# A two-layer decoder step: late gates from SBUF, key-value weights ahead of the norm's root, fewer products for the first sum of squares, denser state steps, outputs in three parts

## The chip, the cores and the metric

The kernel runs on one core of a Trainium2 chip. The metric is device time in microseconds (us) of one execution; lower is better. PE is TensorE (matrix products), DVE is VectorE, ACT is ScalarE, POOL is GpSimd, SP is SyncE, which issues most of the DMAs.

## The reference

One inference step of a hybrid trunk of two layers, for a prompt of 256 tokens behind 16 meta tokens and for 8 single-token samples: 280 columns in all, model width 2048, branch width 4096. Layer A is RWKV-7 time mixing, layer B sliding-window attention with grouped heads; both read one shared key and value. Cut to what the change touches:

```python
def rmsnorm(x, g):
    xf = x.astype(jnp.float32)
    y = xf * lax.rsqrt(jnp.mean(xf * xf, axis=-1, keepdims=True) + RMS_EPS)
    return (y * g.astype(jnp.float32)).astype(x.dtype)
...
    y = (y - mean) * lax.rsqrt(var + GN_EPS) * gn_g.astype(f32).reshape(hn) + gn_b.astype(f32).reshape(hn)
    y = y + jnp.sum(r_h * k_h * r_k.astype(f32), axis=-1, keepdims=True) * v_h
    y = y.reshape(B, T, WIDTH).astype(dt) * jax.nn.silu(z)
    return y @ w_out, S_fin.astype(S0.dtype), xn[:, -1]
...
    kv = (rmsnorm(h, kv_norm) @ w_kv).reshape(B, T, 2, N_KV_HEADS, HEAD_DIM)
    return rotary(kv[:, :, 0], pos), kv[:, :, 1]
...
    y_prompt = rmsnorm(hp, final_norm)[:, N_META:]
    y_sample = rmsnorm(hs, final_norm)
```

The step also returns the new RWKV state of each sample, S x decay - sa x b + v x k, here called a state step.

## The kernel before

Activations lie transposed: model rows on the 128 partitions, the 280 columns along the free axis. KT = 16 tiles of 128 rows make the model width. Matrices are multiplied in three fp32r products, high by high, high by low and low by high (mm3, L205). A weight comes in units of 256 KB (two k tiles by 256 columns): SP loads raw, ACT casts whi (L184), DVE subtracts to get wlo (L186). The buffers of raw, whi and wlo are five units deep, so PE can be some units behind the loads. gemm (L211) runs two units at a time over two banks, one for each 128 columns.

*Order.* In layer A a planner (drive, L591) merges the products with the other streams on PE by written numbers; in the late gates, out_a, phase_b and out_b a scheduler sets the order of each engine ahead of time from the written order and its own costs. At run time each engine's queue is strictly in order: an instruction that waits holds up all behind it.

*Start.* phase0 (L294) squares the 16 tiles of x, adds some squares on DVE and sums the rest over partitions by fp32 products with ones into ps_ssq (L324). A fp32 product counts as two instructions in the profile. Ln and Exp on ACT (L346, L347) give rsb; every first product of PE depends on it. Products of a constant (ps_fill, L320) surround the sums.

*Late gates.* group_norm (L1219) finishes four heads' rows at a time: the bonus tile vT (name 'bonus', two tiles of 272 prompt columns each) takes the normed y (L1237), and SP stores it to yd in DRAM (L1240). gate_a (L1350) loads blocks of 4 x 280 back as gy. For blocks 6 and 7, whose z comes late, it also loads gz from zd, copies the samples' columns from ys (L1362) and multiplies gy with gz on DVE (L1364). gate_tiles splits gy into ghi (ACT) and glo (DVE). At that time PE works on the output projection's first part (ps_o, weights oa1), whose sums into xr (L766, DVE) free its banks. The gates themselves are first used one column later, in out_a.

*out_a* (L1385) runs 8 column pairs of 8 units. After each pair hT is summed (L1404), and kvh, kvl, the parts of the key-value input, are made. Beside it run the state steps of the samples: plan_states gives to each of 12 tiles a unit at which it is computed on DVE (state_step, five instructions); its load is seven units earlier, its store 14 later. The norm's root rb needs the sum of squares of all of hT (ps_sta, L1414): Ln and Exp at L1416 and L1417. Then phase_b multiplies w_kv; bmh and bml (L1424, L1425) are the next layer's inputs, cosr and sinr carry rb into the rotated keys (rout_k, L1651).

*Tail.* out_b (L1800) transposes the last h back (ps_h, L1828), multiplies by the final norm's weight into ht (L1831), sums the squares by ps_stb (L1834), takes a root on DVE (rsf, L1839 and L284 to L288) and scales and stores: 128 prompt rows by DVE and SP (L1844, L1845), 128 by ACT and its own queue (L1846, L1847), the 8 samples last.

## Time and profile before

| what | us |
|---|---|
| three runs | 2165.62, 2161.58, 2156.39 |
| median | 2161.58 |
| the profiled execution | 2157.39 |
| its span (granted TensorE clock 0.993) | 2155.6 |
| DVE busy | 1709.1 |
| ACT busy | 1260.4 |
| DMA moved | 448.52 MB, mean 208 GB/s |

The page shows the busy time of each engine, then the span in 40 slices, the DMA queues, the chain of work that ended last, and the costliest groups. The chain of the whole run is 59% PE. A timeline row gives start and length in us, the engine, the source line, the operation, the tile written and the tiles read, the shape, how many of them, and in brackets how long the engine idled before it and for whom. In the late-gate stage PE stops at 1300.4 us; the root of the key-value norm stands at 1418.9, the last product at 2143.8.

### The profile page before, as it was taken

The numbers are of one execution on the slowest core, as the hardware profiler recorded it, in microseconds if no ns is written. First come the engines' busy times: TensorE is split into PE (matmuls) and PEld (weight loads), VectorE is DVE, ScalarE is ACT, GpSimd is POOL, SyncE is SP. The second block draws the span as 40 slices with busy tenths as digits, with TensorE's granted clock in tenths as the row PEclk, the third lists the DMA queues.
The fourth block names the chain that finished last, engine by engine and source line by source line (L and its number), as shares of the span: only waits on it lengthen the run. The fifth ranks groups of instructions, "written<-read, shape, count | busy, mean of one in ns | idle before, by whom it ended". The sixth has DMA issues, their size and how long they took to land.

```text
span 2155.6 us, 56147 instructions
## 1 busy us (share of the span) xinstructions
PE 2102.4 (98%) x21556; PEld 2001.5 (93%) x21556; DVE 1709.1 (79%) x4115; ACT 1260.4 (58%) x2756; POOL 136.4 (6%) x196
## 2 busy tenths in 40 slices
PE   9999999999999999999999999999999999999997
PEld 7999999999898898889989999999999999999997
DVE  7867867787587777888988787897888888878885
ACT  3457756576666666767666444565565565544443
POOL 0011100001010010100101000100000000000000
PEclk9999999999999999999999999999999999999999
DMA  7997667768666775677655778767545444577774
GB/s 252 310 331 244 197 197 237 207 191 274 200 177 183 249 231 168 208 217 205 199 159 199 242 231 250 238 198 232 149 136 167 153 148 137 170 216 239 230 222 133
DMA packets 277445, 448.52 MB, mean 208 GB/s; under 512 B 53352, under 2 KB 99112, under 8 KB 276784
## 3 DMA queue, kind: packets, MB, share of 16 engines
q1 hardware_dynamic: 276888, 443.89, 66.1%
q8 instruction: 169, 2.77, 0.5%
q10 hardware_dynamic: 288, 1.05, 0.1%
q14 instruction: 100, 0.82, 0.1%
HBM read 382.81 MB, written 66.15 MB: 208 GB/s over the span
## 4 chain that ended last, share of the span: by engine, by line
PE 59%; DVE 4%; DMA 2%; ACT 2%; issue 2%; SPq 0%; DVEq 0%; POOLq 0%; ACTq 0%
PE ps_z L207 5%; PE ps_z L208 5%; PE ps_z L209 5%; PE ps_ob L209 3%; PE ps_ob L208 3%; PE ps_ob L207 3%; PE ps_q L207 3%; PE ps_q L209 3%; PE ps_q L208 3%; PE ps_oa L208 2%; PE ps_oa L207 2%; PE ps_oa L209 2%; PE ps_o L207 1%; PE ps_o L209 1%; PE ps_o L208 1%
## 5 line engine op out<-in xcount | busy, mean ns | idle before, releaser
L207 PE MATMUL ps_z<-mhlm,whi_z 128*128 128x280 f32 x512 | 158.2, 309 | 1.1 <-ACT st L771 1.1
L207 PE MATMUL ps_q<-bmh,whi_qb 128*128 128x264 f32 x512 | 149.9, 293 | 0.1
L208 PE MATMUL ps_z<-mhlm,whi_z 128*128 128x280 f32 x512 | 149.6, 292 | 0.0
L209 PE MATMUL ps_z<-mhlm,wlo_z 128*128 128x280 f32 x512 | 149.5, 292 | 0.0
L207 PE MATMUL ps_z<-bmh,whi_zb 128*128 128x264 f32 x512 | 147.5, 288 | 0.0
L209 PE MATMUL ps_q<-bmh,wlo_qb 128*128 128x264 f32 x512 | 145.7, 285 | 0.6 <-DVE wlo_qb L186 0.6
L208 PE MATMUL ps_q<-bml,whi_qb 128*128 128x264 f32 x512 | 145.6, 284 | 0.0
L208 PE MATMUL ps_z<-bml,whi_zb 128*128 128x264 f32 x512 | 145.4, 284 | 0.0
L209 PE MATMUL ps_z<-bmh,wlo_zb 128*128 128x264 f32 x512 | 145.4, 284 | 0.0
L207 PE MATMUL ps_ob<-ghi,whi_ob 128*128 128x264 f32 x512 | 145.2, 284 | 0.0
L209 PE MATMUL ps_ob<-ghi,wlo_ob 128*128 128x264 f32 x512 | 144.8, 285 | 0.0
L208 PE MATMUL ps_ob<-glo,whi_ob 128*128 128x264 f32 x512 | 144.5, 283 | 0.0
L184 ACT CAST whi_ob<-raw_ob 128x512 fp32r<-128x512 f32 x128 | 79.2, 621 | 97.0 <-PE ps_ob L208 80.3
L184 ACT CAST whi_oa<-raw_oa 128x512 fp32r<-128x512 f32 x128 | 79.0, 620 | 89.7 <-PE ps_oa L208 27.1
L186 DVE TENSOR_TENSOR wlo_r<-raw_r,whi_r 128x512 fp32r<-128x512 f32 x128 | 87.2, 686 | 46.9 <-ACT whi_r L184 44.1
L207 PE MATMUL ps_v<-mhlm,whi_v 128*128 128x280 f32 x384 | 120.7, 314 | 0.0
L207 PE MATMUL ps_k<-mhlm,whi_k 128*128 128x280 f32 x384 | 120.1, 313 | 0.0
L184 ACT CAST whi_v<-raw_v 128x512 fp32r<-128x512 f32 x128 | 78.7, 618 | 64.0 <-PE ps_v L208 35.0
L184 ACT CAST whi_zb<-raw_zb 128x512 fp32r<-128x512 f32 x128 | 78.3, 620 | 62.5 <-PE ps_z L208 38.5
L186 DVE TENSOR_TENSOR wlo_v<-raw_v,whi_v 128x512 fp32r<-128x512 f32 x128 | 87.3, 687 | 34.8 <-ACT whi_v L184 31.2
L186 DVE TENSOR_TENSOR wlo_k<-raw_k,whi_k 128x512 fp32r<-128x512 f32 x112 | 76.7, 690 | 46.7 <-ACT whi_k L184 45.8
L186 DVE TENSOR_TENSOR wlo_oa<-raw_oa,whi_oa 128x512 fp32r<-128x512 f32 x128 | 87.1, 688 | 32.5 <-ACT whi_oa L184 29.5
(461 smaller groups left out, 7747.3 us busy)
## 6 DMA issues: line engine op xcount, KB each, us to landing
raw_k<-a_w_rkvz SPq DMA_DIRECT2D x128, 256.0 KB
raw_v<-a_w_rkvz SPq DMA_DIRECT2D x128, 256.0 KB
raw_r<-a_w_rkvz SPq DMA_DIRECT2D x128, 256.0 KB
raw_z<-a_w_rkvz SPq DMA_DIRECT2D x128, 256.0 KB
raw_oa<-a_w_out SPq DMA_DIRECT2D x128, 256.0 KB
raw_qb<-b_w_qz SPq DMA_DIRECT2D x128, 256.0 KB
raw_zb<-b_w_qz SPq DMA_DIRECT2D x128, 256.0 KB
raw_ob<-b_w_o SPq DMA_DIRECT2D x128, 256.0 KB
```

Source lines behind the costliest of these rows:

```text
L184: self.nc.scalar.copy(hi, src)
L186: return self.nc.vector.tensor_tensor(lo, src, hi.bitcast(F32), op=ALU.subtract)
L207: mm(ps, wh, xh, start=start, stop=False)
L208: mm(ps, wh, xl, start=False, stop=False)
L209: return mm(ps, wl, xh, start=False, stop=stop)
```

## The change

Five parts. (1) phase0: three more sums of squares on DVE (tiles 12 and 13, 8 and 10 with 9 and 11, 14 and 15), so that 8 products instead of 12 go into ps_ssq; ACT squares tiles 14 and 15 together. (2) For blocks 6 and 7 vT is neither stored nor read back: DVE multiplies gz with the vT tiles in SBUF, two tiles at a time, and with ys. (3) The plan of the states in out_a is [10, 16, .. 58, 74, 81, 88] instead of [12, 19, .. 89]. (4) The first three units of w_kv are written ahead of Ln and Exp of rb. (5) In the tail the sums of the last tile are written ahead of the transposes; the last 128 columns of ht are made straight from PSUM with the root; the prompt's outputs are stored in parts of 512, 768 and 768 columns instead of two of 1024.

```diff
 
-    def gemm(self, w, name, nk, col, x, n=N, ncol=256, per=2):
+    def gemm(self, w, name, nk, col, x, n=N, ncol=256, per=2, units=None):
 
...
         out = [p[:min(128, ncol), :n] for p in ps]
-        units = self.wunits(w, name, nk, col, ncol, per)
+        units = units or self.wunits(w, name, nk, col, ncol, per)
 
...
         vsq = lambda a, b: V.tensor_tensor(sq[:, a:b], xn[:, a:b, :N], xn[:, a:b, :N], op=MU)
-        add = lambda a, b: V.tensor_tensor(sq[:, a:a + 2], sq[:, a:a + 2], sq[:, b:b + 2], op=AD)
+        add = lambda a, b, n=2: V.tensor_tensor(sq[:, a:a + n], sq[:, a:a + n], sq[:, b:b + n], op=AD)
         pss, junk = (self.bank(self.pe, n) for n in ("ps_ssq", "ps_fill"))
...
             for k in ks:
-                nc.tensor.matmul(pss[:, :N], ones, sq[:, k], start=k == 0, stop=k == KT - 1)
+                nc.tensor.matmul(pss[:, :N], ones, sq[:, k], start=k == 0, stop=k == KT - 2)
 
...
             vsq(10, 12)
-            summed(8, 9, 10, 11)
             asq(12, 13)
             vsq(13, 14)
-            summed(12, 13)
-            asq(14, 15)
-            vsq(15, 16)
-            summed(14, 15)
+            add(12, 13, 1)
+            summed(12)
+            add(8, 10)
+            summed(8, 9)
+            asq(14, 16)
+            add(14, 15, 1)
+            summed(14)
             A.activation(rsb, pss[:, :N], AF.Ln, scale=1.0 / D, bias=self.epst)
...
                                    op0=MU, op1=AD)
-            if j % 2:
+            if j % 2 and o < GZ // 2:
                 nc.sync.dma_start(self.yd[u // 2][:, 2 * (u % 2):2 * (u % 2) + 2, :L], b[:, :, :L])
...
             z = pool.tile([128, 4, N], F32, tag="gz", bufs=bufs, name=f"gz{b}")
-            nc.sync.dma_start(y[:, :, :L], self.yd[b][:, :, :L])
             nc.sync.dma_start(z, self.zd[b])
...
         if late:
-            nc.vector.tensor_copy(y[:, :, L:N], ys)
-            for pl in range(4):
-                nc.vector.scalar_tensor_tensor(y[:, pl], z[:, pl], 0.5, y[:, pl], op0=ALU.mult, op1=ALU.mult)
+            nc.vector.scalar_tensor_tensor(y[:, :, L:N], z[:, :, L:N], 0.5, ys, op0=ALU.mult, op1=ALU.mult)
+            for i in range(2):
+                s, v = slice(2 * i, 2 * i + 2), self.U[2 * b + i]['bonus']
+                nc.vector.scalar_tensor_tensor(y[:, s, :L], z[:, s, :L], 0.5, v[:, :, :L], op0=ALU.mult, op1=ALU.mult)
         else:
...
         self.wx = self.wx0
-        self.plan_states(self.st0, 0, range(12, 96, 7), 5)
+        self.plan_states(self.st0, 0, [*range(10, 60, 6), 74, 81, 88], 5)
         ones = pool.tile([128, 128], F32, name="ones")
...
                                  stop=k == KT - 1)
+        units = self.wunits(self.I['w_kv'][0], "kv", KT, 0, 256, 2)
+        self.kvu = itertools.chain([next(units) for _ in range(3)], units)
         nc.scalar.activation(self.rb, pst[:, :N], AF.Ln, bias=self.epst, scale=1.0 / D)
...
                 if c % 2 == 0:
-                    pss = self.gemm(I['w_kv'][0], "kv", KT, c * 128, x)
+                    pss = self.gemm(I['w_kv'][0], "kv", KT, c * 128, x, units=None if c else self.kvu)
                     self.pump(c == 2)
...
 
+    def stb(self, pst, rows, a, one, first):
+        for i, r in enumerate(rows):
+            self.nc.tensor.matmul(pst[i][:r, 0:2], a[:, 128 * i:128 * i + r], one, start=first, stop=not first)
+
     def out_b(self):
...
             pt = self.bank(self.pe, f"ps_h2_{k}")
+            if k == KT - 1:
+                self.stb(pst, rows, sq, one, False)
             for i, r in enumerate(rows):
                 nc.tensor.transpose(pt[:r, 128 * i:128 * i + 128], h[:, 128 * i:128 * i + r], self.ident)
-            for i, r in enumerate(rows):
+            for i, r in enumerate(rows[:3 if k < KT - 1 else 0]):
                 s = slice(128 * k, 128 * k + 128)
                 V.tensor_tensor(ht[i][:r, s], pt[:r, 128 * i:128 * i + 128], fn[:r, s], op=ALU.mult)
-            if k >= KT - 2:
-                for i, r in enumerate(rows):
-                    nc.tensor.matmul(pst[i][:r, 0:2], (acc if k == KT - 2 else sq)[:, 128 * i:128 * i + r], one,
-                                     start=k == KT - 2, stop=k == KT - 1)
+            if k == KT - 2:
+                self.stb(pst, rows, acc, one, True)
         rs = pool.tile([128, 3], F32, name="rsf")
...
         outs = (O['y_prompt'][0, 0:128], O['y_prompt'][0, 128:256], O['y_sample'].rearrange("b o d -> (b o) d"))
-        for c in range(2):
-            s = slice(D // 2 * c, D // 2 * c + D // 2)
-            V.tensor_scalar(ht[0][:, s], ht[0][:, s], rs[:, 0:1], None, op0=ALU.mult)
-            nc.sync.dma_start(outs[0][:, s], ht[0][:, s])
+        last = slice(D - 128, D)
+        scaled = lambda i, s: V.tensor_scalar(ht[i][:, s], ht[i][:, s], rs[:, i:i + 1], None, op0=ALU.mult)
+        ends = lambda i, r: V.scalar_tensor_tensor(ht[i][:r, last], pt[:r, 128 * i:128 * i + 128], rs[:r, i:i + 1],
+                                                   fn[:r, last], op0=ALU.mult, op1=ALU.mult)
+        for a, b in ((0, 512), (512, 1280), (1280, 2048)):
+            s = slice(a, min(b, D - 128))
+            scaled(0, s)
+            if b == D:
+                ends(0, 128)
+            nc.sync.dma_start(outs[0][:, a:b], ht[0][:, a:b])
             A.activation(ht[1][:, s], ht[1][:, s], AF.Copy, scale=rs[:, 1:2])
-            nc.scalar.dma_start(outs[1][:, s], ht[1][:, s])
-        V.tensor_scalar(ht[2][:NS], ht[2][:NS], rs[:NS, 2:3], None, op0=ALU.mult)
+            if b == D:
+                ends(1, 128)
+            nc.scalar.dma_start(outs[1][:, a:b], ht[1][:, a:b])
+        V.tensor_scalar(ht[2][:NS, :D - 128], ht[2][:NS, :D - 128], rs[:NS, 2:3], None, op0=ALU.mult)
+        ends(2, NS)
         nc.sync.dma_start(outs[2], ht[2][:NS])
```

What this does to the queues. The first place is the end of the last column but one of ps_o, on DVE, where the late gates are made. Names: wlo_oa1 are weight splits of the output projection, vT14 and vT15 the bonus tiles of block 7, gy6 and gy7 the gates, xr1_12 the sum that frees the banks. Before:

```order
L186 TENSOR_TENSOR wlo_oa1_1536_14_20368<-raw_oa1_1536_14_20365,whi_oa1_1536_14_20367 128x512
L1237 SCALAR_TENSOR_TENSOR vT15_17457<-ps_yt7_3_20353,par_79,vT15_17457 128x272
L186 TENSOR_TENSOR wlo_oa1_1792_0_20386<-raw_oa1_1792_0_20383,whi_oa1_1792_0_20385 128x512
L186 TENSOR_TENSOR wlo_oa1_1792_2_20417<-raw_oa1_1792_2_20414,whi_oa1_1792_2_20416 128x512
L186 TENSOR_TENSOR wlo_oa1_1792_4_20442<-raw_oa1_1792_4_20439,whi_oa1_1792_4_20441 128x512
L766 TENSOR_TENSOR xr1_12_20229<-ps_o_1536_0_20227,xr1_12_20229 128x280
L766 TENSOR_TENSOR xr1_12_20229<-ps_o_1536_1_20228,xr1_12_20229 128x280
L1364 SCALAR_TENSOR_TENSOR gy6_20340<-gz6_20341,gy6_20340 128x280 x4
L186 TENSOR_TENSOR glo6_20350<-gy6_20340,ghi6_20349 128x1120
L186 TENSOR_TENSOR wlo_oa1_1792_6_20448<-raw_oa1_1792_6_20445,whi_oa1_1792_6_20447 128x512
```

After, from the first gate of block 7 on (the three products of block 6 stand just before):

```order
L1364 SCALAR_TENSOR_TENSOR gy7_20386<-gz7_20387,ys_234 128x4x8
L1367 SCALAR_TENSOR_TENSOR gy7_20386<-gz7_20387,vT14_16628 128x2x272
L187 TENSOR_TENSOR wlo_oa1_1536_14_20359<-raw_oa1_1536_14_20356,whi_oa1_1536_14_20358 128x512
L1240 SCALAR_TENSOR_TENSOR vT15_17455<-ps_yt7_3_20345,par_79,vT15_17455 128x272
L187 TENSOR_TENSOR glo6_20342<-gy6_20335,ghi6_20341 128x1120
L187 TENSOR_TENSOR wlo_oa1_1792_0_20377<-raw_oa1_1792_0_20374,whi_oa1_1792_0_20376 128x512
L1367 SCALAR_TENSOR_TENSOR gy7_20386<-gz7_20387,vT15_17455 128x2x272
L187 TENSOR_TENSOR wlo_oa1_1792_2_20405<-raw_oa1_1792_2_20402,whi_oa1_1792_2_20404 128x512
L187 TENSOR_TENSOR wlo_oa1_1792_4_20430<-raw_oa1_1792_4_20427,whi_oa1_1792_4_20429 128x512
L769 TENSOR_TENSOR xr1_12_20225<-ps_o_1536_0_20223,xr1_12_20225 128x280
L769 TENSOR_TENSOR xr1_12_20225<-ps_o_1536_1_20224,xr1_12_20225 128x280
L187 TENSOR_TENSOR glo7_20393<-gy7_20386,ghi7_20392 128x1120
```

The products of the gates and glo6 have moved ahead of the xr sums; behind these follows glo7 at once.

On ACT the same place, with the casts of the weights (whi) and of the gates (ghi). Before:

```order
L184 CAST whi_oa1_1536_14_20367<-raw_oa1_1536_14_20365 128x512
L184 CAST whi_oa1_1792_0_20385<-raw_oa1_1792_0_20383 128x512
L184 CAST whi_oa1_1792_2_20416<-raw_oa1_1792_2_20414 128x512
L184 CAST whi_oa1_1792_4_20441<-raw_oa1_1792_4_20439 128x512
L184 CAST ghi6_20349<-gy6_20340 128x1120
L184 CAST whi_oa1_1792_6_20447<-raw_oa1_1792_6_20445 128x512
```

After:

```order
L185 CAST whi_oa1_1536_14_20358<-raw_oa1_1536_14_20356 128x512
L185 CAST ghi6_20341<-gy6_20335 128x1120
L185 CAST whi_oa1_1792_0_20376<-raw_oa1_1792_0_20374 128x512
L185 CAST whi_oa1_1792_2_20404<-raw_oa1_1792_2_20402 128x512
L185 CAST whi_oa1_1792_4_20429<-raw_oa1_1792_4_20427 128x512
L185 CAST ghi7_20392<-gy7_20386 128x1120
L185 CAST whi_oa1_1792_6_20435<-raw_oa1_1792_6_20433 128x512
```

ghi6 has moved ahead of three weight casts, and ghi7, which stood behind the whole column, now stands ahead of the cast of unit 6.

The second place is ACT behind the table load for the root's Exp (rb). bmh are inputs of layer B, whi_kv casts of w_kv. Before:

```order
L1417 ACT_TABLE_LOAD
L1417 ACTIVATE rb<-rb 128x280
L1424 ACTIVATE bmh_22815<-hT,par 128x280
L1424 ACTIVATE bmh_22819<-hT,par 128x280
L1424 ACTIVATE bmh_22823<-hT,par 128x280
L184 CAST whi_kv_14_22156<-raw_kv_14_22154 128x512
L1424 ACTIVATE bmh_22827<-hT,par 128x280
L184 CAST whi_kv_0_22227<-raw_kv_0_22225 128x512
L1424 ACTIVATE bmh_22831<-hT,par 128x280
L1424 ACTIVATE bmh_22835<-hT,par 128x280
L1424 ACTIVATE bmh_22839<-hT,par 128x280
```

After:

```order
L1422 ACT_TABLE_LOAD
L1422 ACTIVATE rb<-rb 128x280
L1429 ACTIVATE bmh_22803<-hT,par 128x280
L1429 ACTIVATE bmh_22807<-hT,par 128x280
L1429 ACTIVATE bmh_22811<-hT,par 128x280
L1429 ACTIVATE bmh_22815<-hT,par 128x280
L185 CAST whi_kv_14_22151<-raw_kv_14_22149 128x512
L185 CAST whi_kv_0_22216<-raw_kv_0_22214 128x512
L1429 ACTIVATE bmh_22819<-hT,par 128x280
L1429 ACTIVATE bmh_22823<-hT,par 128x280
L1429 ACTIVATE bmh_22827<-hT,par 128x280
```

Only one bmh has changed place with the cast of unit 14; the rows ahead of the table load (nine bmh, Ln, the cast of unit 12) are as before.

The third place is the end of DVE's queue. ps_stb holds the sums of squares, rsf the root, ps_h_15 the last transposed tile. Before:

```order
L1831 TENSOR_TENSOR ht_30009<-ps_h_14_32654,fn 8x128
L1831 TENSOR_TENSOR ht_30007<-ps_h_15_32668,fn 128x128
L1831 TENSOR_TENSOR ht_30008<-ps_h_15_32668,fn 128x128
L1831 TENSOR_TENSOR ht_30009<-ps_h_15_32668,fn 8x128
L1839 TENSOR_SCALAR rsf<-ps_stb_30010 128x1
L1839 TENSOR_SCALAR rsf<-ps_stb_30011 128x1
L1839 TENSOR_SCALAR rsf<-ps_stb_30012 8x1
L284 TENSOR_SCALAR rsy<-rsf 128x3
```

After, at the same place, and from the root on:

```order
L1842 TENSOR_TENSOR ht_29997<-ps_h_14_32642,fn 8x128
L1848 TENSOR_SCALAR rsf<-ps_stb_29998 128x1
L1848 TENSOR_SCALAR rsf<-ps_stb_29999 128x1
L1848 TENSOR_SCALAR rsf<-ps_stb_30000 8x1
L285 TENSOR_SCALAR rsy<-rsf 128x3
```

```order
L289 SCALAR_TENSOR_TENSOR rsf<-rst,rsy 128x3
L1852 TENSOR_SCALAR ht_29995<-ht_29995,rsf 128x512
L1852 TENSOR_SCALAR ht_29995<-ht_29995,rsf 128x768
L1852 TENSOR_SCALAR ht_29995<-ht_29995,rsf 128x640
L1853 SCALAR_TENSOR_TENSOR ht_29995<-ps_h_15_32656,rsf,fn 128x128
L1853 SCALAR_TENSOR_TENSOR ht_29996<-ps_h_15_32656,rsf,fn 128x128
L1865 TENSOR_SCALAR ht_29997<-ht_29997,rsf 8x1920
L1853 SCALAR_TENSOR_TENSOR ht_29997<-ps_h_15_32656,rsf,fn 8x128
```

The three products with ps_h_15 have moved behind the root, and the scale of 1024 columns has become three of 512, 768 and 640. On PE nothing moves there.

More of the change, by code (lines that the diff above doesn't have):

```diff
@@ L2 @@
 import functools
+import itertools
 import numpy as np
```

## The prediction

> **What bounds the kernel now.** I read the page first: its span, and the busy time of each engine.
>
> ```profile
> span 2155.6 us, 56147 instructions
> PE 2102.4 (98%) x21556; PEld 2001.5 (93%) x21556; DVE 1709.1 (79%) x4115; ACT 1260.4 (58%) x2756; POOL 136.4 (6%) x196
> ```
>
> TensorE (PE) is busy for 98% of the span and the change leaves its number of rows as it was but for four products at the start. So what can be won is PE's waits, time at a lowered clock, and the two ends, where nothing else hides a delay. Next I read the waits of PE between 1290 and 1480 us, where three of the five parts lie (line, what it waited for: total us, times, longest).
>
> ```profile
> PE ps_o L207 <- ACT whi_oa L184: 2.0, 1, 2.0
> PE ps_kv L207 <- ACT whi_kv L184: 1.6, 2, 1.4
> ...
> PE ps_o L209 <- DVE wlo_oa L186: 0.9, 1, 0.9
> PE ps_kv L207 <- DVE rout_k L1651: 0.7, 1, 0.7
> PE ps_o L207 <- DVE xr L766: 0.5, 1, 0.5
> ```
>
> Then the windows of 20 us (length, busy us of PE, PEld, DVE, ACT, POOL with counts, granted clock, DMA share, GB/s).
>
> ```profile
> 1280.00:1300.00 20.00, 19.55 (x154) 19.32 (x153) 12.70 (x26) 6.76 (x10) 0.00 (x0) 1.00 1.03 347
> 1300.00:1320.00 20.00, 17.09 (x111) 16.64 (x110) 13.33 (x22) 9.84 (x15) 0.00 (x0) 0.83 0.82 267
> ...
> 1360.00:1380.00 20.00, 20.00 (x157) 20.00 (x157) 18.92 (x31) 10.47 (x20) 4.42 (x4) 1.00 0.82 253
> ...
> 1420.00:1440.00 20.00, 17.72 (x133) 17.05 (x133) 19.37 (x44) 14.66 (x30) 0.53 (x1) 1.00 0.60 183
> ```
>
> The late-gate stage is the second row: 111 products, against 157 in a full window, at a granted clock of 0.83. The chain of waits says why:
>
> ```profile
> 1291.32 4.91 DMA gy<-yd
> ...
> 1299.14 1.54 DVE gy L1364 x4
> 1300.70 1.13 ACT ghi L184
> ```
>
> The gate of block 6 is read back from DRAM; VectorE (DVE) multiplies it only when it is there, and ScalarE (ACT) casts it to ghi ahead of the weight cast for which PE waits.
>
> **Late gates: what goes.** PE's timeline over the hole:
>
> ```profile
> 1296.28 0.40 PE L207 MATMUL ps_o<-mhlm,whi_oa 128*128 128x280 f32 x1 [0.45 <-DVE xr L766]
> 1296.51 0.29 PE L208 MATMUL ps_o<-mhlm,whi_oa 128*128 128x280 f32 x1
> ...
> 1300.12 0.29 PE L209 MATMUL ps_o<-mhlm,wlo_oa 128*128 128x280 f32 x1
> 1302.40 0.40 PE L207 MATMUL ps_o<-mhlm,whi_oa 128*128 128x280 f32 x1 [1.99 <-ACT whi_oa L184]
> 1302.64 0.29 PE L208 MATMUL ps_o<-mhlm,whi_oa 128*128 128x280 f32 x1
> 1303.84 0.60 PE L209 MATMUL ps_o<-mhlm,wlo_oa 128*128 128x280 f32 x1 [0.92 <-DVE wlo_oa L186]
> 1304.24 0.43 PE L207 MATMUL ps_o<-mhlm,whi_oa 128*128 128x280 f32 x1
> ...
> 1309.61 0.31 PE L209 MATMUL ps_o<-mhlm,wlo_oa 128*128 128x280 f32 x1
> ```
>
> From 1296.51 to 1300.12 a product takes 3.61/28 = 0.129 us from start to start. The next starts 2.28 us later, 2.15 more than the pitch; 1302.64 to 1303.84 is 1.20, that is 1.07 too much. Then 1304.24 to 1309.61 holds 23 steps of 0.233: 0.104 lost on each, 25 times with the two at its edges, 2.6 us. If the gate stands in no queue any more, 2.15 + 1.07 + 2.6 = 5.8 us go.
>
> *What comes instead.* DVE's queue, as it runs now:
>
> ```profile
> 1288.48 0.17 DVE L1362 COPY gy<-ys 128x32 f32<-128x32 f32 x1
> ...
> 1291.15 0.69 DVE L186 TENSOR_TENSOR wlo_oa<-raw_oa,whi_oa 128x512 fp32r<-128x512 f32 x1 [0.25 <-ACT whi_oa L184]
> 1293.25 0.69 DVE L186 TENSOR_TENSOR wlo_oa<-raw_oa,whi_oa 128x512 fp32r<-128x512 f32 x1 [1.41 <-ACT whi_oa L184]
> 1295.17 0.69 DVE L186 TENSOR_TENSOR wlo_oa<-raw_oa,whi_oa 128x512 fp32r<-128x512 f32 x1 [1.23 <-ACT whi_oa L184]
> 1295.78 0.80 DVE L766 TENSOR_TENSOR xr<-ps_o,xr 128x280 f32<-128x280 f32 x2
> ...
> 1301.86 1.32 DVE L186 TENSOR_TENSOR glo<-gy,ghi 128x1120 fp32r<-128x1120 f32 x1 [1.19 <-ACT ghi L184]
> ```
>
> In the order of after, these stand ahead of the xr sum that frees PE's bank: four products of 544 columns (half of the 1.54 us of four times 280, less an edge: 0.68 each, 2.7 in all) and the glo of block 6 (1.3). That is 4.0 us more work before 1295.78. DVE idles 0.25 + 1.41 + 1.23 = 2.9 us there, waiting for casts of weights that load late while the DMA share is 1.03. The new work is ready inside these idles (the products from 1288.48, glo after a cast of 1.13 behind them), so I take them as filled, even with no load sooner: xr comes 4.0 - 2.9 = 1.1 us later, and the wait before 1296.28 grows by about **1.0 us**. Bounds: 0, if the four stores of 272 KB and two loads of 544 KB that go bring the casts forward, and +4.0, if no idle is filled. One column on, a fourth split of the column after, wlo_oa_6 (0.69), now stands ahead of the xr sum too; its bank has some lead, so 0.3 us (0 to 1.0). ACT has no such edge: ghi of both blocks stands early, behind gates that are ready. In all -5.8 + 1.0 + 0.3 = **-4.5 us** (-0.8 to -5.8).
>
> The new gates also wait for gz. SP's waits between 1286 and 1289 us show where its two issues behind the second gz load stood:
>
> ```profile
> SPq L200 <- DMA gz<-zd: 2.5, 2, 1.6
> ```
>
> Both gz tiles are thus there before 1289. DVE comes to block 6's first gate product at 1288.48 and to block 7's some 3 us later, so I charge nothing; a us that gz came later would be a us of the whole queue.
>
> Row and rule on the clock: the wait of 1.4 us for whi_kv lies in the window 1420 to 1440, whose clock stays 1.00; the stage with 2.15 and 1.07 us of holes falls to 0.83. I therefore charge no clock to an xr wait of some 1.6 us. [...]
>
> **Start.** The first sum of squares hangs on PE:
>
> ```profile
> 7.92 1.10 DVE L313 TENSOR_TENSOR dx<-xn 128x560 f32<-128x560 f32 x2
> 8.06 4.98 PE L324 MATMUL ps_ssq<-dx,ones 128*128 128x280 f32 x20 [0.29 <-DVE dx L314]
> 9.32 0.44 ACT L312 ACTIVATE dx<-xn 128x280 f32<-128x280 f32 x1 [0.33 <-DMA xn<-xT]
> 13.08 0.49 ACT L346 ACTIVATE rsb<-ps_ssq,epst 128x280 f32<-128x280 f32 x1 [3.32 <-PE ps_ssq L324]
> ```
>
> Ten fp32 products (two records each) take 4.98 us, 0.5 each; the Ln follows at once, and all work up to PE's first weights hangs on it. Six of the ten stay. Without waits they end at 8.06 + 3.0 = 11.1. The added sums: DVE is done with its squares at 9.02, then add(12,13) of one tile (about 0.4) and add(8,10) of two (about 0.7) end at 10.1; the square of 14 and 15 starts at 9.32, is done about 10.0, their sum about 10.5. So PE has product 12 at 9.45, 8 and 9 from 10.15, 14 at 11.15 to 11.65. The Ln moves from 13.08 to 11.7: **-1.4 us** (-1.0 with one more wait, -2.0 without any).
>
> **Key-value root and states.**
>
> ```profile
> 1424.93 0.45 DVE L1454 TENSOR_TENSOR cosr<-cs,rb 128x280 f32<-128x280 f32 x1 [0.63 <-ACT rb L1417]
> ```
>
> The written order changes, the order on ACT hardly: Ln, nine bmh, table load and Exp stand as before, and behind Exp one cast, whi_kv_14, now has a fourth bmh (0.45 us) ahead of it. That can lengthen the first wait for whi_kv (1.4 of the 1.6 us), but the last one, for rout_k (0.7), decides: the chain from Exp over cosr to rout_k on DVE, with as many instructions as before. **0** (-0.5 to +0.8, the cast's delay and the edge of a us in the waits). The denser state steps fill DVE: in the full windows of out_a it is busy up to 18.92 of 20 us, PE 20.00. A state is five instructions on 128x512, as the weight splits above (0.69 with its end, an estimated 0.61 apart): 3.0 us. One state in six units instead of seven adds 3.0/42 = 0.07 us of DVE to each unit of twelve products (1.55 us), 5%. The split weights lie ahead of PE and cover it: **0**. If that cover is gone, the 5% are 5.0 us over out_a's 64 units, of which DVE's free 1.1 in 20 us takes most: up to +1.5.
>
> **Tail.**
>
> ```profile
> 2143.34 0.68 DVE L1831 TENSOR_TENSOR ht<-ps_h,fn 128x128 f32<-128x128 f32 x3 [0.68 <-PE ps_h L1828]
> 2143.95 0.27 DVE L1839 TENSOR_SCALAR rsf<-ps_stb 128x1 f32<-128x1 f32 x3
> ...
> 2146.22 1.42 DVE L1844 TENSOR_SCALAR ht<-ht,rsf 128x1024 f32<-128x1024 f32 x2
> 2147.00 1.01 SPq L1845 DMA_DIRECT2D y_prompt<-ht  x2
> ```
>
> ```profile
> 2148.00:2149.00 1.00, 0.00 (x0) 0.00 (x0) 0.82 (x1) 0.40 (x1) 0.00 (x0) 0.50 1.01 406
> ...
> 2152.00:2153.00 1.00, 0.00 (x0) 0.00 (x0) 0.00 (x0) 0.00 (x0) 0.00 (x0) 0.50 1.08 410
> ```
>
> From 2148 on the outputs leave at 400 GB/s with the DMA full, so the end moves with the first issue. That stands behind a scale of 1024 columns (1.42/2 = 0.71); with 512 it is 0.36 shorter. rsf no longer waits behind three ht products; PE's own sums end near it, so I give 0.15 (0 to 0.6). **-0.5 us** (-0.1 to -1.0). The pieces that follow come sooner than 256 KB leave (0.65 us at 400 GB/s).
>
> [...]
>
> **The sum**: -4.5 - 1.4 + 0 + 0 - 0.5 = **-6.4 us**. The profiled execution took 2157.39 us (span 2155.6 and 1.8 around it), so 2151.0 by that. It lies 4.2 under the median of 2161.58, and the runs reach from 2156.39 to 2165.62; I carry the difference over: 2161.58 - 6.4 = **2155.2 us**. A run-to-run spread of 9 us is as large as the gain; 0.5%, 10.8 us, is about what a measurement here can tell from no change.
>
> **Rivals.**
>
> - *The hole moves to xr* (0.16). Half of DVE's idle stays empty, because ghi's cast and the weights' casts come in bunches: 1.45 more on xr, a hole of some 3 us, and the clock falls as it does now (2.6). Gates: -4.5 + 1.45 + 2.6 = -0.45, the sum -0.45 - 1.9 = -2.35: **2159.2**. For it: this edge has no slack already (0.5 us for xr). Against: the window before it has DVE busy 12.70 of 20 us only.
> - *More than counted* (0.14). Gates -5.8, start -2.0, tail -1.0, root -0.5, the ends of the bounds: -9.3, **2152.3**. For it: 2.2 MB leave a stage with a DMA share of 1.03. Against: it needs four good ends at once.
> - *Slower: the state steps hold up hT* (0.07). PE writes its two banks in turn, twelve products a time, so the sum hT that frees the first has 12 x 0.129 = 1.55 us. In five of the eight columns a state's instructions stand right ahead of it, before in three. Where DVE comes over 1.55 us late, PE waits; from 6.4/5 = 1.3 us in each of the five the gain is gone, and with the whole step's 3.0 us: 2161.6 - 6.4 + 15 = **2170.2**. For it: DVE at 18.92 of 20. Against: PE stands at 20.00 in that window now, with steps ahead of hT in the same queue.
> - *The outputs pay for each piece* (0.03). The span ends 2155.6 - 2153.0 = 2.6 us after the last full DMA window; were that paid once for each piece instead of once, two more on a queue cost 5.2: -6.4 + 5.2, **2160.4**. Against it, the queues kept 400 GB/s across the border of two halves.
> - *The change doesn't do what it says*: for the key-value weights that is so by the order, and it is in the sum as 0.
>
> **How the numbers follow.** The forecast has 0.60, and its own range, from the bounds that are likely together, is 2153 to 2158. The range reaches from 2148 (the rival with more, and some 4 us of the runs' spread) to 2161 (the hole at xr, the outputs by pieces, and a little spread); the slower rival and the outer parts of the others stay out. Faster by over 0.5% means under 2150.8: less than half of the rival with more and the forecast's lower runs, 0.14. Slower by over 0.5% means over 2172.4, a part of the slower rival: 0.04. Within: 0.82.
>
> **What would show it.** Late gates: no wait of PE for whi_oa or wlo_oa near 1300, a wait for xr of 1 to 2 us in its place, and a clock near 1.00 in that window; one of 3 us with a clock under 0.95 shows the first rival. Start: the Ln at 11.7, and every later row of phase A earlier by 1.4. Root: waits for whi_kv and rout_k about as now. States: no wait of PE for hT or wlo_oa up to the root. Tail: first issue 0.5 us sooner after the last product, and 400 GB/s without a break. The forecast is wrong if the profiled span is not 5 to 8 us shorter, or if it is by other stages than these.

## The result, and the profile after

| | before | changed |
|---|---|---|
| five runs, us | 2165.62, 2161.58, 2156.39, 2162.57, 2159.31 | 2142.43, 2149.97, 2149.5, 2149.89, 2143.14 |
| median | 2161.58 | 2149.5 |
| profiled execution (its span) | 2157.39 (2155.6) | 2142.43 (2140.6) |

The ratio of the times is 0.9942, 95% interval 0.9925 to 0.9959: faster by 12.1 us, where 6.4 were forecast. The profiled execution is the fastest of its five, so two pages set side by side show more than that, 15.0.

The page of the changed kernel, its first rows:

```profile
span 2140.6 us, 56118 instructions
PE 2097.5 (98%) x21548; PEld 1998.3 (93%) x21548; DVE 1710.2 (80%) x4114; ACT 1261.0 (59%) x2757; POOL 137.7 (6%) x196
```

Its waits of PE from 1270 to 1480 us (line, what it waited for: total us, times, longest):

```profile
PE ps_kv L208 <- ACT whi_kv L185: 1.7, 1, 1.7
PE ps_kv L208 <- DVE rout_k L1656: 0.5, 1, 0.5
PE ps_kv L210 <- DVE wlo_kv L187: 0.5, 1, 0.5
PE ps_o L208 <- DVE xr L769: 0.3, 1, 0.3
```

The waits for whi_oa and wlo_oa (2.0 and 0.9) are gone; the wait for xr, expected to grow to some 1.6, is 0.3; the root has about what it had. The windows (length, busy us of PE, PEld, DVE, ACT, POOL, clock, DMA share, GB/s):

```profile
1280.00:1300.00 20.00, 19.68 (x153) 19.46 (x152) 15.94 (x27) 10.05 (x15) 0.00 (x0) 1.00 0.99 311
1300.00:1320.00 20.00, 20.00 (x157) 20.00 (x156) 14.50 (x25) 9.70 (x17) 1.84 (x2) 1.00 0.71 219
...
1340.00:1360.00 20.00, 20.00 (x157) 20.00 (x157) 19.63 (x32) 10.29 (x18) 3.02 (x3) 1.00 0.75 232
```

The products that stood in before's window from 1300 to 1320, at a clock of 0.83, start 7.6 us sooner here and take 13.9 us, from 1292.5 to 1306.5, across both first rows, whose clock is 1.00. In the last row DVE does its denser state steps, 19.63 of 20 us, and PE stands at 20.00 beside it. The timeline of DVE at the gates:

```profile
1280.50 1.35 DVE L1367 SCALAR_TENSOR_TENSOR gy<-gz,vT 128x544 f32<-128x544 f32 x2
...
1284.53 1.31 DVE L187 TENSOR_TENSOR glo<-gy,ghi 128x1120 fp32r<-128x1120 f32 x1
...
1287.00 1.28 DVE L187 TENSOR_TENSOR wlo_oa<-raw_oa,whi_oa 128x512 fp32r<-128x512 f32 x2
1288.20 0.79 DVE L769 TENSOR_TENSOR xr<-ps_o,xr 128x280 f32<-128x280 f32 x2
```

No row from 1280.39 to 1288.92 has an idle time in brackets: the new work fills all the idles of DVE, and PE waits only 0.3 us for xr.

Where 15.0 us of the two pages lie, product by product of PE: 1.1 at the start; 6.3 in layer A up to the last columns of ps_o; 6.2 in the late gates; 1.1 from out_a to the first heads of layer B; 0.3 behind the last product. The 6.3 were in no term of the forecast, and the experiments are mostly about them.

### The profile page after: what moved, and what is told of

It is laid out like the page before. It is cut to its first block, busy times and chain, and to the rows that moved or that the text cites. A ratio compares the mean times of both kernels' runs of the same rounds, so it can differ in the third digit from the quotient of the medians.

```text
span 2140.6 us, 56118 instructions
## 1 busy us (share of the span) xinstructions
PE 2097.5 (98%) x21548; PEld 1998.3 (93%) x21548; DVE 1710.2 (80%) x4114; ACT 1261.0 (59%) x2757; POOL 137.7 (6%) x196
## 4 chain that ended last, share of the span: by engine, by line
PE 86%; DVE 5%; DMA 4%; ACT 2%; issue 1%; SPq 0%; POOL 0%; DVEq 0%; POOLq 0%; ACTq 0%
PE ps_z L208 6%; PE ps_z L209 6%; PE ps_z L210 6%; PE ps_r L208 3%; PE ps_k L208 3%; PE ps_ob L210 3%; PE ps_ob L209 3%; PE ps_ob L208 3%; PE ps_v L208 3%; PE ps_r L209 3%; PE ps_q L208 3%; PE ps_k L209 3%; PE ps_r L210 3%; PE ps_v L210 3%; PE ps_q L210 3%; PE ps_v L209 3%
## 5 line engine op out<-in xcount | busy, mean ns | idle before, releaser
L208 PE MATMUL ps_k<-mhlm,whi_k 128*128 128x280 f32 x384 | 120.2, 313 | 0.0
L210 PE MATMUL ps_k<-mhlm,wlo_k 128*128 128x280 f32 x384 | 112.5, 293 | 0.0
L209 PE MATMUL ps_k<-mhlm,whi_k 128*128 128x280 f32 x384 | 112.5, 293 | 0.0
```

The costliest lines, as they stand in the source:

```text
L208: mm(ps, wh, xh, start=start, stop=False)
L209: mm(ps, wh, xl, start=False, stop=False)
L210: return mm(ps, wl, xh, start=False, stop=stop)
```

## Experiments

Ratios are to the kernel before on the same chip, with 95% intervals. "By the means" is against 2159.4 us, the mean of all runs of before on record, so it can differ from the ratio by a us or so; a ± is one standard error. A single profile of layer A can't be compared with another: three profiles of one program (before, before_copy, kv_only) give 1190.6, 1198.2 and 1194.8 us from product 400 to the first product of column 1536 of ps_o. The start, out_a, the keys and the tail repeat to 0.3 us in these three; the gate stage (47.8, 45.8 and 46.6 us) does not, and layer B differs by 0.6.

**The start alone** (start_only): before, with part 1 of the change.

```diff
-            summed(8, 9, 10, 11)
...
+            add(8, 10)
+            summed(8, 9)
```

> The kernel before with the first part alone (three more sums of squares on DVE, 8 products instead of 12 for ps_ssq). Aligned product by product, the changed kernel's profiled execution gained 1.1 us at the start, 6.3 in layer A behind it, 6.2 in the late gates, 1.1 between out_a and the keys, 0.3 in the tail. Theory by places: the gain of layer A is the spread of executions; this kernel gains 1.1 us at the start and nothing else that repeats: ratio 0.9995, at most 0.998. Rival: the earlier start, with the eight or so instructions of ACT and DVE that change places in layer A through it, gains there too: 4 to 7 us in all, ratio 0.9965 to 0.998.

0.9973 (0.9958 to 0.9988), 4.3 us by the means, about four times what is won at the start: PE's first product of ps_k comes 1.0 us sooner (16.11 for 17.09); some 3 us come behind it.

**The gates alone** (gates_only): before, with part 2.

```diff
-            if j % 2:
+            if j % 2 and o < GZ // 2:
...
-            nc.sync.dma_start(y[:, :, :L], self.yd[b][:, :, :L])
```

> The kernel before with the second part alone (gates of blocks 6 and 7 from SBUF). Theory by places: PE's hole near 1300 us and the low clock behind it go, a wait for xr of 0.3 to 1 us stays: 6.2 us shorter in that stage, ratio about 0.997. Rival (the prediction's own size): 4.5 us, with a longer wait for xr. Layer A before the gates should differ from the kernel before only by chance, up to some 5 us either way.

0.9953 (0.9936 to 0.9970), 8.3 us by the means against 4.5 forecast. Its one profile has the forecast's first rival: the waits of PE there, then two windows.

```profile
PE ps_o L207 <- DVE xr L766: 2.0, 1, 2.0
```

```profile
1280.00:1300.00 20.00, 17.96 (x139) 17.74 (x138) 16.49 (x29) 8.69 (x12) 0.00 (x0) 0.98 0.95 318
1300.00:1320.00 20.00, 20.00 (x147) 20.00 (x147) 10.40 (x16) 9.09 (x15) 0.00 (x0) 0.93 0.76 242
```

Why xr came late there, on ACT (its timeline):

```profile
1294.08 0.62 ACT L184 CAST whi_oa<-raw_oa 128x512 fp32r<-128x512 f32 x1 [2.87 <-DMA raw_oa<-a_w_out]
1296.01 0.62 ACT L184 CAST whi_oa<-raw_oa 128x512 fp32r<-128x512 f32 x1 [1.32 <-DMA raw_oa<-a_w_out]
```

Two weights landed late, so DVE idled ahead of the split that stands before xr. That a row waits for the one ahead of it in its queue is seen in before's timeline of DVE: a row of rsty (L287) follows the one that it reads (L286) by 0.22 us at 343.01, but by 2.96 at 347.75, where a split between the two (wlo_v at 347.14) had waited 2.17 us for its cast. The 320 products of the gate stage took 44.85 us here, 41.3 to 41.7 in the five other profiles with this part (wait for xr 0 to 0.4), and 44.5 to 48.0 in the eight without it.

**All but the start** (no_start): the changed kernel with the start of before.

```diff
-            add(8, 10)
-            summed(8, 9)
...
+            summed(8, 9, 10, 11)
```

> The changed kernel with the first part taken back; its order of instructions in layer A is that of the kernel before. Theory by places: 6.2 + 1.1 + 0.3 = 7.6 us faster than before, ratio 0.9965, and 1.1 us slower than the changed kernel. Rival (the start's change also gains in layer A): only the same 7.6 us here, but 4 to 7 us slower than the changed kernel, whose ratio was 0.9942: this run then stands at 0.9965 and the changed kernel well below it. If the start part alone stands at 0.9995 and this at 0.9945, the gain of layer A has another cause.

0.9958 (0.9938 to 0.9978), mean 2150.9; the sixteen runs of the changed kernel, after_copy and no_plan have 2145.5. So the start is worth 5.4 ± 1.6 us in the full change too, as far as runs on several chips can be compared (the mean of before differs by some 2 us between them), and within that error the parts add up.

**The kernel before again** (before_copy), nothing edited.

> The kernel before, unchanged, for a second profile of it. Theory by places: stage by stage it differs from the first profile in layer A by some us either way and by under 0.3 us in every other stage. Rival: layer A repeats within 1 us, and the changed kernel's 6.3 us there are its own.

One run, 2163.3 us; layer A is 7.7 us longer than in the first profile. The gate stage, against the expectation, is 1.9 us shorter; the other stages are alike.

**The key-value weights alone** (kv_only): before, with `units=None if c else self.kvu` and the three units taken ahead of the root.

> The kernel before with the fourth part alone (first three units of w_kv written ahead of the root). Every engine's order of instructions is the same as before's, row by row, so this is also the measure of how two runs of one program differ. Theory: ratio 1.000 with an interval of some 0.0015 to either side, a wait for whi_kv of 1.4 to 1.5 us and for rout_k of 0.7 us as before, each stage outside layer A within 0.3 us. Rival: the gains of 2 to 4 us that start alone and gates alone show beyond their stages come from the comparison itself (the kernel before runs slower than any other); then this stands at 0.998 to 0.999 too.

1.0000 (0.9988 to 1.0012). The rows of every engine are those of before, so this is the same program under another name: part 4's written order does nothing.

**The plan of the states alone** (plan_only).

```diff
-        self.plan_states(self.st0, 0, range(12, 96, 7), 5)
+        self.plan_states(self.st0, 0, [*range(10, 60, 6), 74, 81, 88], 5)
```

> The kernel before with the third part alone (states from unit 10, one in six units, the ninth ahead of the root). Theory by places: in out_a nothing (PE full before and after), between the first product of w_kv and of layer B some 0.6 us less, because bml and the splits behind the root no longer wait behind a state's instructions, and 0.4 in the first heads of layer B: 1.0 us, ratio 0.9995. Rival (the prediction): 0, the chain from Exp to rout_k as long as before.

0.9996 (0.9982 to 1.0011). From the first ps_kv to the first ps_q it takes 56.27 us against 56.90; the four profiles with this plan and bmh left alone have 56.27 to 56.29, the nine with the old plan 56.86 to 56.90. Between the two pages, PE's waits at the root sum to 3.3 us in before and 2.7 in the changed kernel. 0.6 us is below what the times tell.

**The tail alone** (tail_only): before, with the sums first, three pieces (`for a, b in ((0, 512), (512, 1280), (1280, 2048))`) and the last 128 columns by themselves.

> The kernel before with the fifth part alone (sums first, outputs in three parts). Theory: the time from the last product to the end falls from 12.0 to 11.7 us and nothing else changes: ratio 0.9998, not told from 1. The prediction said 0.5. Rival (each piece pays for itself): 12.0 or more.

0.9997 (0.9983 to 1.0012); from the start of the last product to the end 11.69 us against 11.99. The tail of the changed kernel, DVE and the issues:

```profile
2128.79 0.49 DVE L1848 TENSOR_SCALAR rsf<-ps_stb 128x1 f32<-128x1 f32 x3 [0.80 <-PE ps_stb L1807]
...
2131.29 1.48 DVE L1852 TENSOR_SCALAR ht<-ht,rsf 128x512 f32<-128x512 f32 x3
...
2131.80 1.58 SPq L1860 DMA_DIRECT2D y_prompt<-ht  x3
```

Its windows behind the first issue:

```profile
2133.00:2134.00 1.00, 0.00 (x0) 0.00 (x0) 1.00 (x3) 0.56 (x1) 0.00 (x0) 0.50 1.01 375
2134.00:2135.00 1.00, 0.00 (x0) 0.00 (x0) 0.66 (x2) 0.00 (x0) 0.00 (x0) 0.50 1.06 358
2135.00:2136.00 1.00, 0.00 (x0) 0.00 (x0) 0.00 (x0) 0.00 (x0) 0.00 (x0) 0.50 1.02 409
```

The issue comes 0.5 us sooner behind scale and products, as forecast; two windows at 358 to 375 GB/s, where before had 397 to 410, take some 0.2 back.

**The changed kernel again** (after_copy), nothing edited.

> The changed kernel, unchanged, for more runs and a second profile. Theory by places: start 15.99, late gates (320 products from the first of the column) 41.6, keys 56.3, end 11.7 us as in its first profile; layer A anywhere between that of its first profile (1184) and the longest seen (1199); median between 2147 and 2152. Rival: layer A repeats the first profile's 1184 within 2 us, and the median stands under 2147.

0.9938 (0.9920 to 0.9956), median 2146.3, a little under what was expected; layer A takes 1187.7 us, so it does not repeat the first profile's 1184 either.

**The start with the old order behind it** (start_f9): start_only, with four more products of the constant ahead of the sums. The start part also moves a few instructions in layer A: two casts whi_r and one whi_z, copies of TT and ET and their neighbours change places on ACT, three pairs on DVE; the last of these places, near 1312 us, lie in the gate stage. With the four products the order is that of before again.

```diff
-            filling(5)
+            filling(9)
```

> The kernel before with the first part and four more products of a constant ahead of the sums, which delay them by some 0.4 us of the 1.1 won. With it ACT and DVE have the order of the kernel before in the whole of layer A, where start alone swaps some eight instructions of ACT and three of DVE. Theory by order: what start alone won beyond its place (4.0 us in all by the means of its runs, 1.1 of them at the start) comes from those swaps: this kernel gains 0.7 us only, ratio 0.9997. Theory by the earlier start: it gains most of the same, 3.5 us, ratio 0.9984. Start: first product of ps_k at 16.3 to 16.5 us instead of 17.1.

1.0001 (0.9986 to 1.0015). ps_k starts 0.6 us sooner than before (17.09), and nothing more is won: being that much early does not bring the 3 us.

```profile
16.46 3.80 PE L242 MATMUL ps_k<-mst,raw_k 128*128 128x280 f32 x15 [0.75 <-DVE mst L376]
```

**The new order without the start** (before_f3): before, with two products of the constant fewer, which makes the same swaps in layer A and a few more.

```diff
-            filling(5)
+            filling(3)
```

> The kernel before with three products of a constant ahead of the first sums instead of five; the sums wait for the squares anyway, so the first product of ps_k should stand at 17.0 to 17.3 us as before. The scheduler, which counts those products, now puts ACT's casts of whi_r (units 12 and 0) and its copies TT and ET in layer A in the order that the first part of the change gives them, and changes a few more places of ACT, DVE and SP there. Theory by order: that alone gains what the first part won behind its place, about 3 us (ratio 0.998 to 0.999), with layer A's profile under 1192 us. Rival: the first part's gain needs the earlier start, or was chance: ratio 1.000 within 0.0015.

0.9987 (0.9972 to 1.0001), 3.0 ± 1.2 us by the means, although in its one profile ps_k starts 1.8 us later than before (18.92, not 17.0 to 17.3 as expected). The interval reaches 1, so this run alone does not exclude the rival; if all its runs start that late, the part behind the start is about 4.8 us shorter. With start_only, which gains, and start_f9, which does not, it points to the swaps; which of them counts is open. Why the start was late is in the timeline and the windows:

```profile
6.70 1.21 PE L324 MATMUL ps_ssq<-dx,ones 128*128 128x280 f32 x4 [2.14 <-DVE dx L314]
...
8.20 6.67 PE L324 MATMUL ps_ssq<-dx,ones 128*128 128x280 f32 x20 [0.29 <-DVE dx L314]
...
18.92 1.45 PE L242 MATMUL ps_k<-mst,raw_k 128*128 128x280 f32 x5 [0.75 <-DVE mst L374]
```

```profile
8.00:12.00 4.00, 3.80 (x9) 2.85 (x10) 1.61 (x4) 1.49 (x3) 0.80 (x3) 0.57 1.05 391
```

A hole of 2.14 us and then ten products in 6.67 us instead of 4.98, at a clock of 0.57.

**All but the plan** (no_plan): the changed kernel with `range(12, 96, 7)`.

> The changed kernel with the states' plan taken back. The late-gate stage took 41.6 us in the profiles with the plan (three) and 44.85 in the one of the gates alone, where a wait of 2.0 us for xr and a lower clock stood. Theory by chance: that wait hangs on when two weight loads land, not on the plan; this stage takes 41.6 to 45 us and the stage of the keys 56.9 instead of 56.3; median within 1 us of the changed kernel's 2146 to 2149 plus 0.6. Rival: the plan is needed for the gates' gain: 44 to 45 us again and a median 3 us above the changed kernel's.

0.9933 (0.9915 to 0.9950), median 2145.16, no slower than the full change; its gate stage is 41.3 us, so the gates don't need the plan.

**Inputs of layer B spread behind the casts** (bm_spread): the changed kernel, with each bmh put behind a cast of the key-value weights, so that Exp follows Ln at once.

```diff
+            for k in range(KT):
+                with self.tc.issue_after(self.his[k - 24].ins):
+                    self.bmx.append(self.norm_mix(bp, "bm", P_BN, k))
```

> The changed kernel with the sixteen bmh of layer B's input each put behind one weight cast of w_kv, from the second column's first on, instead of nine between Ln and Exp of the root and seven behind. Theory: what PE waits for at the root (whi_kv 1.7, rout_k 0.5, wlo_kv 0.5 us in the changed kernel) hangs on ACT's queue, where 3.9 us of bmh stand between Ln and Exp and 1.8 more ahead of the cast: the three waits go, the stage from the first product of w_kv to the first of layer B falls from 56.3 to 53.9 us, ratio to before some 0.0011 below the changed kernel's. Rival: the bmh and bml then crowd DVE's queue with the states' instructions and new waits for wlo_kv take their place: 56 us or more.

0.9954 (0.9936 to 0.9972), no better than the change. The wait for whi_kv at the root is gone, and the waits of PE between 1400 and 1480 us are now others:

```profile
PE ps_s L1675 <- DVE q L1661: 2.3, 1, 2.3
PE ps_kv L209 <- DVE rout_k L1660: 1.7, 1, 1.7
PE ps_kv L211 <- DVE wlo_kv L187: 1.3, 2, 0.8
```

The stage takes 57.63 us instead of 56.3.

**What the swaps do, from the fourteen traces.** The waits of PE from 15 to 1170 us whose releaser is "issue", that is, nothing that the profile shows; first start_f9 (old order), then start_only (new):

```profile
PE ps_z L208 <- issue: 2.6, 1, 2.6
PE ps_so L1087 <- issue: 1.8, 3, 1.0
PE ps_r L209 <- issue: 1.6, 1, 1.6
PE ps_so L1081 <- issue: 1.0, 1, 1.0
```

```profile
PE ps_so L1087 <- issue: 1.2, 2, 0.8
PE ps_r L208 <- issue: 0.2, 1, 0.2
```

The DMA queue q8 of the kind "instruction" moves pieces of 16 KB, 169 in a run of before, beside PE's 43,112 products and weight loads: 255 for each piece. A piece lands every 13 us or so, yet all 70 such holes of 0.2 us or more in the fourteen traces end 1.23 to 1.60 us after one has landed. The author's reading is that PE has run out of instructions there; no run shows that by itself. In layer A up to block 6 the eight traces with the old order have 4.3 to 6.9 us of these holes (mean 5.5), the six with the new order 1.2 to 5.1 (mean 2.95). The difference of 2.5 us is near the 3 of the runs, but that it makes them is not shown: the profile of start_only has the fewest of these holes (1.2) and still the longest layer A (1199.3), with 37.6 us at half clock.

The second thing that varies is the clock. From the start of layer A to the last product, the fourteen traces have 88 spells at half clock, each 3.41 us or twice that long, and each within 3.41 us of at least 1.09 us of idle PE; 79 holes of over 1.0 us were followed by none. Layer A of the three profiles of one program, with the holes and spells up to its end (us):

| | layer A | holes without releaser | at half clock | A less holes less half of that |
|---|---|---|---|---|
| before | 1190.6 | 5.6 | 13.7 | 1178.1 |
| before_copy | 1198.2 | 7.5 | 27.3 | 1177.0 |
| kv_only | 1194.8 | 6.5 | 23.9 | 1176.3 |

7.7 us of spread become 1.8. These three are a lucky choice, though: plan_only, tail_only and start_f9 have the same order in layer A and come to 1180.3, 1179.5 and 1174.0 in this way, so that the six keep 6.3 us of spread. PE's waits for ACT, DVE and POOL vary too. With all of PE's idle time taken off, whoever ended it, and half of the time at half clock, the fourteen traces lie between 1148.6 and 1152.8 us, where layer A itself takes 1184.2 to 1199.3. All this is read from traces; no run changed PE's supply of instructions by itself, and which of the swaps moves it was not tried.

**The same at block 6.** PE's run of small products ps_so in the stage ahead of the gates, first before, then gates_only:

```profile
1195.40 0.76 PE L1085 MATMUL ps_so<-TR,ET 32*16 32x16 f32 x70
1197.17 0.65 PE L1085 MATMUL ps_so<-TR,ET 32*16 32x16 f32 x58 [1.01 <-issue]
```

```profile
1196.30 1.24 PE L1085 MATMUL ps_so<-TR,ET 32*16 32x16 f32 x128
```

The queues at the time of the piece of q8 that lands ahead of the end of before's hole, and of the same piece in gates_only (packets, MB, share), before from 1194.6 to 1195.8, then gates_only from 1194.4 to 1195.6:

```profile
q1 hardware_dynamic: 322, 0.43, 102.0%
q8 instruction: 1, 0.02, 5.8%
```

```profile
q1 hardware_dynamic: 143, 0.25, 57.8%
q8 instruction: 1, 0.02, 5.7%
```

In before, with block 6's two vT stores issued at 1188.25 and 1191.85, data fill the DMA engines (102.0%; 57.8% in gates_only), and the piece starts 0.8 us ahead of the run (1194.63); without them it starts 1.8 us ahead (1194.47). In the eight traces with the stores it starts at most 0.8 us ahead, once behind; in the six without them 0.9 to 2.1. The hole is 1.0 to 2.2 us in all eight traces with the stores, with a spell at half clock behind it in six; 0 to 0.6 us in the six without them, and no spell. The stretch of 1220 products takes 83.4 us on average with the stores and 81.1 without.

## Why the prediction was right or wrong

The median of 2149.5 lies in the range of 2148 to 2161, in part by luck: of the 12 us, some 5 (2.3 and 3 below) come from steps that the sum does not have. The forecast's own sign of being wrong came true: the profiled span is not 5 to 8 us shorter but 15.0, and half of that lies in stages that it did not name.

- **Late gates**, -4.5: the mechanism was right. The size at its place came out too, but by two errors that cancel. The gate stage has 46.3 us on average in the eight profiles without the part and 41.3 to 41.7 in five of the six with it, so -4.7 (-4.2 with the sixth, gates_only). The 5.8 us of waits and low clock went, but the page they were read from has 47.8 us there, near the top of the eight, 1.5 over their mean; and the 1.0 for xr did not come in those five, where its bound of 0 held. gates_only has the other case, 2.0 us and the lower clock, so the forecast's first rival does come when two weights land late. Not priced at all were the two stores of block 6, which left a stage before the one looked at: another -2.3. The sum counted "four stores and two loads" in the gates' own stage alone.
- **The clock of a short hole**: the forecast charged none to a wait of 1.6 us, since the root's wait of 1.4 leaves the window at 1.00. That step falls: it was read from one execution. The same wait in kv_only, which is the same program, in its windows and its waits:

```profile
1420.00:1440.00 20.00, 18.39 (x126) 17.76 (x125) 19.37 (x43) 15.91 (x31) 0.56 (x2) 0.91 0.59 184
```

```profile
PE ps_kv L208 <- ACT whi_kv L185: 1.6, 2, 1.4
PE ps_kv L210 <- DVE wlo_kv L187: 0.3, 1, 0.3
```

The hole is caught here, at 0.91; a spell at half clock stands behind the root in six traces of fourteen. Yet at the root it costs nothing, 56.87 us against 56.90: the slower PE waits less for DVE. The wait for rout_k (0.7) is gone, and that for wlo_kv was longer in before:

```profile
PE ps_kv L209 <- DVE wlo_kv L186: 1.0, 2, 0.7
```

In the gate stage it does cost: gates_only, with its 2.0 us hole and a spell, takes 3.2 to 3.6 us more than the five others. The traces show spells of 3.41 and 6.83 us, which in each trace all start on one grid of 3.413 us (to 0.002), at another place in each trace; by this, whether a hole is caught hangs on where it falls, as with the same wait at 1.00 in before and 0.91 in kv_only. A mean price of a hole that may be caught was the right charge, where PE sets the pace behind it.
- **Start**, -1.4: at its place 1.1. In the timeline of the changed kernel DVE's three sums end at 10.56, about as put in (10.5), but the four products behind them start at 9.61, not 9.45, and end at 11.94, not 11.65: 0.58 each, not 0.5. So the Ln is at 11.98, not 11.7:

```profile
9.10 1.46 DVE L315 TENSOR_TENSOR dx<-dx 128x280 f32<-128x280 f32 x3
...
9.61 2.33 PE L325 MATMUL ps_ssq<-dx,ones 128*128 128x280 f32 x8 [0.36 <-DVE dx L315]
...
11.98 0.49 ACT L349 ACTIVATE rsb<-ps_ssq,epst 128x280 f32<-128x280 f32 x1 [2.00 <-PE ps_ssq L325]
```

  The step that failed is "every later row of phase A earlier by 1.4": layer A was taken as shifted, though its order had changed in several places. Behind the start another 3 to 5 us were won (start_only, before_f3), and none where the old order stood behind an earlier start (start_f9); by what mechanism is open.
- **Root and states**, 0: the key-value weights 0, as said; the states cost nothing and bring 0.6 at the root. The slower rival, hT held up, had its condition, DVE at 19.63 of 20 us, but out_a took 99.3 us in every profile but tail_only's (99.9), which has the old plan.
- **Tail**, -0.5: -0.3. The issue came 0.5 sooner; the rate of the first two us was not priced. A cost for each piece, the 2.6 us of the rival, did not show. Three pieces for two are also one more on each queue, not two as the prediction counted: 2.6 us were at stake, not 5.2, and the tail ended 0.3 us sooner.

The terms as measured, with 3 for the order in layer A: -4.7 - 2.3 - 1.1 - 3 - 0.6 - 0.3 = -12.0, beside 12.1 by the medians. So close an agreement is luck: the 3 alone has a standard error of 1.2.

## What to carry to other kernels

Where a change edits one place and the order of instructions differs elsewhere too, those places belong at least in the range. A stage that spreads by 3 us between profiles is not sized from one page. A removed transfer is to be priced at each place where it stood, above all where the DMA is full (102.0% here) and an engine runs through many short instructions (1220 products here). A hole of one to three us on PE should be charged with its own length and, by chance and where PE sets the pace behind it, half of a spell at half clock (half of 3.41 or 6.83 us here); and a serial stage that spreads by 15 us between profiles is compared by many runs, not by two profiles.

## What was not expected of the hardware

- PE idles where the profile shows nothing that it waits for: 70 holes of up to 3.1 us, all ending 1.23 to 1.60 us behind a piece of 16 KB on the queue "instruction". That it waits there for its own instructions is the author's reading, which no run shows.
- From the start of layer A to the last product, half clock came in 88 spells of 3.41 or 6.83 us behind holes from 1.1 us on, and the same hole was caught in one execution (kv_only, 0.91) and not in another (before, 1.00). This and PE's idle time of every kind make most of the spread of layer A (15 us, 4 without them).
- With two products of a constant fewer at the start, the one profile has the whole start 1.8 us later (first ps_k at 18.92 for 17.09).
